# Bounds of the second MLP weights from sums of squares, taken in the first product, and more low pieces of u on GpSimd

## The chip, the cores and the metric

The kernel runs on one core of one Trainium2 chip. The metric is the device time of an execution in microseconds. A core has TensorE (PE, with its weight loads PEld), VectorE (DVE), ScalarE (ACT), GpSimd (POOL) and SyncE (SP), whose queue issues nearly all DMAs here. Each engine works through its own instructions in the order in which they were written down when the program was built.

## The reference

One block of a streaming encoder over x of 1024 x 1024: RMSNorm, two groups of attention heads, an output projection with residual, and then the part that the change is about:

```python
n2 = rms_norm(h, norm2_g[layer])                       # 1024 x 1024
u = jnp.square(jax.nn.relu(jnp.einsum('bsd,df->bsf', n2, w_ff1[layer])))   # 1024 x 4096
h = h + jnp.einsum('bsf,fd->bsd', u, w_ff2[layer])     # 4096 -> 1024
return rms_norm(h, final_norm_g)
```

All inputs and the output are float32. The kernel may compute in another way as long as the output agrees.

## The kernel before, in words

The attention and the output projection take the first 440 us or so and are not touched. The rest is the MLP, in two products.

Both products multiply 2 x 2 blocks with seven block products instead of eight (Strassen's scheme in Winograd's form), numbered p = 1 to 7. Each float32 operand of a block product is split into a high and a low fp16 piece, and `mm3` makes three matmuls of them: high x high, high x low, low x high. So that the pieces fit into fp16, an operand is first multiplied by a power of two. For that power the kernel needs a bound of the absolute values before it can split anything.

**First product** (`prepare1`, `product1`, order in `order1`). The 4096 columns of w1 are cut in NQ = 8 blocks n of 512. Per block, four tiles `w` of 128 x 1024 are loaded (`load1`), `see1` takes the largest absolute value of each (VectorE, L1161), `scale1` spreads the largest over the partitions by a TensorE transpose (`all_w`), makes the power of two, and ScalarE scales the four tiles (L1328). `prepare1` forms the combination T of two tiles (VectorE, L1335), `split` casts the high piece W (ScalarE, L1361) and takes the low piece (GpSimd or VectorE, L1363), two steps ahead of its use. `product1` then issues 24 matmuls a step (u blocks, k, three pieces) at two-output tiles, copies or sums the partial products (tiles k and v; ScalarE L1409 to L1421, VectorE L1417 to L1433), squares the relu and stores the seven operands of u to DRAM (`ud`, by `put`), from where the second product reads them back. The stores are sent by SyncE during the next step.

**Second product** (`prepare2`, `product2`, order in `order2`). The 4096 rows of w2 are cut in four groups g of two blocks n (GQ = 2), so a group has 14 steps of 24 matmuls: p in the order 1, 5, 6, 3, 7, 2, 4, each for both n. `load2w` loads the eight w2 tiles of a group, `see2` takes the largest absolute value of each (VectorE, L1161), and for groups 1 to 3 the largest goes through DRAM (`write`, `read`: SyncE sends 512 bytes out and loads them back on all partitions) to `scale2`. For group 0 it is spread by TensorE at the end of the first product. `fetch2` loads u tiles four steps ahead into six tiles that take turns (`load2u`: three of the stage ring "ws", three of "tst"). `prepare2` is written two steps ahead of the matmuls: ScalarE casts the high piece U, and for p in 1, 2, 3, 4 scales u first and has GpSimd subtract (L1363); for p in 5, 6, 7 VectorE scales and subtracts in one operation (L1365). For w2, VectorE forms the combination Z (L1335), ScalarE casts V (L1361), VectorE takes the low piece (L1365). When a pair of steps is done, `add_up` adds a PSUM bank to the float32 accumulator C (VectorE, L1652), and the next product into that bank waits for it.

All TensorE instructions stand in program order, and so do SyncE's. The order on VectorE, ScalarE and GpSimd is set by a scheduler when the program is built, from its own idea of how long things take; at run time nothing overtakes on an engine.

Of the kernel before, what the change touches and what calls it, by code (L numbers as in the profile page):

```python
# [17 lines left out]
P = 128  # L18
# [30 lines left out]
P_UP = 14  # L49
PLACES = ((4, 0, 6, 12), (0, 10, 20, 30))  # L50
V_UP = 13
PAD = 80
X_UP, W_UP, U_UP = 7, 12, 11


# [1 line left out]
def kernel(  # L57
# [40 lines left out]
    def page(shape, name, dt=F32R):  # L98
        return main.tile(shape, dt, tag="pg", bufs=NPAGES, name=name)
# [1049 lines left out]
    class Top:  # L1149
# [10 lines left out]
        def see(self, src):  # L1160
            nc.vector.tensor_reduce(self.column(), flat(src), mybir.AxisListType.X, ALU.max, apply_absolute_value=True)  # L1161

        def gather(self):
            assert self.count == self.n
            self.top = small.tile([P, 1], F32, tag="top", bufs=3, name=f"top_{self.name}")
            nc.vector.tensor_reduce(self.top, self.cols[:, : self.n], mybir.AxisListType.X, ALU.max)
# [153 lines left out]
    def scale1(n):  # L1320
        top1[n].spread()
        e = top1.pop(n).bits()
        up1 = power(scale_tile("up1", str(n), 2), e, -1.0, 254 + W_UP)
        down1[n] = power(scale_tile("down1", str(n), 3), e, 1.0, -W_UP)
        nc.vector.tensor_tensor(down1[n], down1[n], xdown, ALU.mult)
        for b in ((0, 0), (0, 1), (1, 1), (1, 0)):
            w = w1s[(n, *b)]
            nc.scalar.activation(w, w, AF.Copy, scale=up1)  # L1328

    def page1(shape, name, dt=F32):  # L1330
        return page(shape, name, dt)
# [173 lines left out]

    def load2w(n, i, j):
        if (n, i, j) not in w2s:
            w2s[n, i, j] = page([P, 2, HALF], f"w2_{n}_{i}{j}", F32)
            src = w_ff2[n * HALF + i * 2 * P : n * HALF + (i + 1) * 2 * P, j * HALF : (j + 1) * HALF]
            queue[0].dma_start(w2s[n, i, j], src.rearrange("(a p) c -> p a c", p=P))  # L1510
        return w2s[n, i, j]

    reads = {
        1: ((0, 0),), 5: ((0, 1), (0, 0)), 6: ((1, 1),), 3: ((1, 1),), 7: ((1, 1), (0, 1)), 2: ((1, 0),), 4: ((1, 0),),
# [15 lines left out]
    top2, up2, uup, udown, down2 = {}, {}, {}, {}, {}  # L1530

    def see2(g, tiles):
        if g not in top2:
            top2[g] = Top(f"w2_{g}", NQ + NQ // GQ + g, 4 * GQ)
        for tile2 in tiles:
            top2[g].see(w2s[tile2])
        if top2[g].count == 4 * GQ:
            top2[g].gather()

    def scale_of_u(g, spread=True):  # L1540
        if spread:
# [3 lines left out]
        udown[g] = power(scale_tile("udown", str(g), 4), e, 2.0, -127 - U_UP)  # L1545

    def scale2(g):
        if g == 0:
            top2[g].spread()
        e = top2.pop(g).bits(-30)  # L1550
        up2[g] = power(scale_tile("up2", str(g), 2), e, -1.0, 254 + W_UP)
        down2[g] = power(scale_tile("down2", str(g), 2), e, 1.0, -W_UP)
        nc.vector.tensor_tensor(down2[g], down2[g], udown[g], ALU.mult)

    ops2, made_b, ready2 = {}, {}, set()

    def prepare2(at):
        if at >= len(order2) or order2[at][1:] in ready2:
            return
        g, p, n = order2[at]  # L1560
        ready2.add((p, n))
        alloc = page if at <= 3 * GQ else page3
        high = lambda name: page16([P, 2, 2, HALF], name, alloc)
        temp = lambda name: alloc([P, 2, HALF], name, F32)
        a = u2s.pop((n, p))
        b = second_operands(lambda i, j: w2s[n, i, j], made_b.setdefault(n, {}), p, f"Z{n}_{p}", dve, temp)
        ops2[n, p] = (
            split(a, f"U{n}_{p}", pool if p in (1, 2, 3, 4) else dve, high, uup[g]), split(b, f"V{n}_{p}", dve, high, up2[g])
        )

    queue[0] = InOrder(nc.sync)
    for at, (n, p) in enumerate(order1):
        if p == (1 if n > 1 else 5) and n:
            load1(n + 1)
        ahead1 = at + (AHEAD1 + 1 if at < AT_ONCE else AHEAD1)

        behind = (n, p) == (0, 2)
# [12 lines left out]
        if p == 3 and n and n % GQ == 0:  # L1590
            scale_of_u(n // GQ - 1)
        if (n, p) in ((NQ - 2, 4), (NQ - 1, 1)):
            for tile2 in blocks2(0)[(p == 1) * 4 :][:4]:
                load2w(*tile2)
        if n == NQ - 1:
            if p in (5, 6):
                see2(0, blocks2(0)[(p == 6) * 4 :][:4])
            if p == 6:
                for i in range(LOAD2 - 1):
                    fetch2(i)  # L1600
            if p == 3:
                scale2(0)
            if p in (7, 2):
                prepare2({7: 0, 2: 1}[p])
    while stores:
        stores.pop(0)()
    mp_.close()
# [112 lines left out]
    for at, (g, p, n) in enumerate(order2[:-GQ]):  # L1720
# [2 lines left out]
        fetch2(at + LOAD2)  # L1723
        step = at % (7 * GQ)
        if g + 1 < NQ // GQ:
            loads = (0, 1, 2, 3) if g else (1, 2, 4, 5)
            if step in loads:
                for tile2 in blocks2(g + 1)[2 * loads.index(step) :][:2]:
                    load2w(*tile2)
            if step - 3 in loads:  # L1730
                see2(g + 1, blocks2(g + 1)[2 * loads.index(step - 3) :][:2])
            if step in (8, 10):
                (top2[g + 1].write if step == 8 else top2[g + 1].read)()
            if step == 12:
                scale2(g + 1)
        if g + 1 == NQ // GQ and step == 0:
            down, up = down2[g], scale_tile("up", "", 1)
            nc.vector.reciprocal(up, down)
        if g == 0 and step in (1, 3, 6):
            last = NQ // GQ - 1  # L1740
            {1: topu[last].write, 3: topu[last].read, 6: lambda: scale_of_u(last, False)}[step]()
        prepare2(at + AHEAD2)
        if at in (0, 1, 3, 9):
            load_acc(*into[{0: 1, 1: 5, 3: 6, 9: 4}[at]])
# [122 lines left out]
```

## Time and profile before

| what | value |
|---|---|
| median of 3 runs (lowest, highest) | 1069.95 us (1069.53, 1072.73) |
| the profiled execution | 1074.07 us, of which the span is 1072.3 |
| mean granted TensorE clock | 0.982 |
| busy: PE, DVE, ACT, POOL | 1009.7, 801.3, 655.4, 402.4 us |
| first product | from about 436 to 746 us |
| second product | from about 746 to 1064 us |
| DMA | 184 MB, mean 172 GB/s |

The page counts busy time per engine over the span, the chain that ended last, and groups of equal instructions with their mean duration and the idle time in front of them ("<-DVE C" means that the wait ended when VectorE had written C). A timeline row gives start, duration, engine, line, operation, output <- inputs, size, count, and in brackets the idle time before it. A row of windows gives, for a stretch, its length and the busy time of PE, PEld, DVE, ACT and POOL with instruction counts, the granted clock, the share of DMA and its GB/s. In the names, `f` is a PSUM tile of the first product, `f_a`, `f_b`, `f_c` are the chains of the second, `tops_w` and `top_w` are the maxima of a weight, `u` is a loaded operand of u, `ud` its place in DRAM.

### The profile page before, as it was taken

To read this page: it belongs to the slowest core of one execution; us is meant where nothing else is said; L and a number is where in the kernel's file an instruction comes from. 1 tells how busy PE (TensorE), PEld (TensorE's weight loads), DVE (VectorE), ACT (ScalarE), POOL (GpSimd) and SP (SyncE) were. 2 spreads that over 40 slices of the span, in tenths; PEclk is the share of its full clock that TensorE was granted. 3 is DMA by queue.
4 is the path that set the end of the run, shared out by engine and by line. 5 is a ranking of instruction groups with operands and counts; after the bars stand their busy time and mean duration, and the time that the engine had idled before them with its cause. 6 is when DMAs were issued, how large, how long until landed. Compare 5 with 4: busy or idle time off the path is not lost. (4 is left out here: it accounts for less than half of the span.)

```text
span 1072.3 us, 13955 instructions
## 1 busy us (share of the span) xinstructions
PE 1009.7 (94%) x4815; PEld 593.6 (55%) x4815; DVE 801.3 (75%) x1293; ACT 655.4 (61%) x1033; POOL 402.4 (38%) x327
## 2 busy tenths in 40 slices
PE   9999999999878999899999999998898799999997
PEld 7888887777656777544444444443343344444443
DVE  5577787877767465895767776777796978979886
ACT  7676766676666757755765566456264545446546
POOL 0466674244344634113533543361042214126113
PEclk9999999999989999899999999998999899999999
DMA  9854538999999954105634552473968557334204
GB/s 351 243 134 119 147 75 190 196 220 194 248 224 257 211 220 145 46 20 177 216 109 147 196 189 89 173 271 121 305 266 231 203 101 269 104 81 138 79 1 157
DMA packets 142726, 184.04 MB, mean 172 GB/s; under 512 B 78656, under 2 KB 96576, under 8 KB 142656
## 3 DMA queue, kind: packets, MB, share of 16 engines
q1 hardware_dynamic: 142512, 182.89, 58.7%
q8 instruction: 38, 0.62, 0.3%
q14 instruction: 32, 0.26, 0.1%
q10 hardware_dynamic: 144, 0.26, 0.1%
HBM read 103.43 MB, written 42.99 MB: 137 GB/s over the span
## 5 line engine op out<-in xcount | busy, mean ns | idle before, releaser
L169 PE MATMUL f<-X,W 128*128 128x512 f16 x1344 | 296.6, 383 | 0.9 <-DVE topf L1419 0.7
L169 PEld LDWEIGHTS <-U 128*128 128x128 f16 x1356 | 133.0, 98 | 186.9 <-issue 26.7
L169 PEld LDWEIGHTS <-W 128*128 128x128 f16 x1344 | 132.4, 99 | 161.6 <-issue 6.7
L169 PE MATMUL f_a<-V,U 128*128 128x512 f16 x756 | 168.2, 381 | 12.8 <-DVE C L1652 9.1
L1363 POOL TENSOR_TENSOR U<-u,U 128x1024 f16<-128x1024 f32 x32 | 78.0, 2444 | 239.9 <-ACT U L1361 137.1
L1363 POOL TENSOR_TENSOR W<-T,W 128x1024 f16<-128x1024 f32 x29 | 63.2, 2180 | 96.6 <-ACT W L1361 96.6
L169 PE MATMUL f_c<-V,U 128*128 128x512 f16 x384 | 86.9, 386 | 9.3 <-DVE C L1652 5.5
L1363 POOL TENSOR_TENSOR W<-w,W 128x1024 f16<-128x1024 f32 x23 | 55.3, 2403 | 84.4 <-ACT W L1361 84.4
L1359 ACT ACTIVATE u<-u,uup 128x1024 f32<-128x1024 f32 x32 | 36.5, 1144 | 74.0 <-DMA u<-ud 72.1
L1161 DVE TENSOR_REDUCE tops_w<-w 128x1 f32<-128x1024 f32 x64 | 75.8, 1208 | 7.2 <-DMA w<-in_w_ff_dram 6.9
L169 PE MATMUL op_A<-w_o,y 128*128 128x512 f32 x192 | 58.8, 434 | 8.5 <-DVE ts_vB L431 5.2
L1361 ACT ACTIVATE W<-T 128x1024 f16<-128x1024 f32 x32 | 33.6, 1050 | 48.6 <-DVE T L1335 48.5
L618 ACT ACTIVATE P_B<-P_B,nm_B 128x640 f32<-128x640 f32 (+2 forms) x64 | 44.2, 691 | 30.2 <-DVE nm_B L615 14.9
L863 DVE SCALAR_TENSOR_TENSOR H_B<-P_B,rc_B,H_B 128x640 f16<-128x640 f32 (+2 forms) x64 | 52.5, 848 | 10.5 <-ACT H_B L858 10.1
L1365 DVE SCALAR_TENSOR_TENSOR V<-Z,up,V 128x1024 f16<-128x1024 f32 x32 | 47.8, 1494 | 12.4 <-ACT V L1361 12.4
L169 PE MATMUL ip_qB<-nT,w_qB 128*128 128x512 f32 x192 | 53.8, 406 | 1.1 <-DVE t_kB L405 1.0
L169 PE MATMUL ip_kB<-nT,w_kB 128*128 128x512 f32 x192 | 53.7, 404 | 0.0
L1361 ACT ACTIVATE V<-Z,up 128x1024 f16<-128x1024 f32 x32 | 36.4, 1138 | 27.0 <-DVE Z L1335 21.8
L169 PE MATMUL ip_vB<-nT,w_vB 128*128 128x512 f32 x192 | 51.2, 400 | 0.0
L169 PE MATMUL ip_qA<-nT,w_qA 128*128 128x512 f32 x192 | 50.3, 396 | 0.4 <-DVE VA L175 0.4
L1420 ACT ACTIVATE k<-k,down 128x1024 f32<-128x1024 f32 x24 | 27.5, 1144 | 37.1 <-DVE topf L1419 37.1
L169 PE MATMUL op_B<-w_o,y 128*128 128x512 f32 x192 | 48.4, 407 | 0.2 <-ACT o L1053 0.2
(276 smaller groups left out, 1996.8 us busy)
## 6 DMA issues: line engine op xcount, KB each, us to landing
w<-in_w_ff_dram SPq DMA_DIRECT2D x64, 512.0 KB, 7.9
u<-ud SPq DMA_DIRECT2D x56, 512.0 KB, 5.9
ud<-k SPq DMA_DIRECT2D x48, 512.0 KB, 3.1
KkB<-t_kB SPq DMA_DIRECT2D x32, 256.0 KB, 5.3
xr<-in_x_dram SPq DMA_DIRECT2D x8, 512.0 KB, 9.3
st_o<-in_w_out_dram SPq DMA_DIRECT2D x8, 512.0 KB, 4.8
h<-in_x_dram SPq DMA_DIRECT2D x8, 512.0 KB, 5.0
hB<-h SPq DMA_DIRECT2D x8, 512.0 KB, 2.6
```

The source lines that it names most:

```text
L169: pe(nc.tensor.matmul(*args, **kw))
L618: nc.scalar.activation(pr, pr, AF.Exp, bias=nm, scale=-1.0, accum_out=sm)
L863: nc.vector.scalar_tensor_tensor(lo, q, rc, hi, ALU.mult, ALU.subtract)
L1161: nc.vector.tensor_reduce(self.column(), flat(src), mybir.AxisListType.X, ALU.max, apply_absolute_value=True)
L1359: nc.scalar.activation(full, full, AF.Copy, scale=up)
L1361: nc.scalar.activation(w[0], full, AF.Copy, scale=1.0 if up is None else up)
L1363: engine.tensor_tensor(w[1], full, w[0], ALU.subtract)
L1365: engine.scalar_tensor_tensor(w[1], full, up, w[0], ALU.mult, ALU.subtract)
L1420: nc.scalar.activation(v, v, AF.Relu, scale=down1[n])
```

## The change

The bounds of w2 are no longer maxima in the second product. From the ninth step of the first product on, `look2` loads the w2 tiles of all four groups one after the other into the stage ring (tiles m), two steps later ScalarE squares a tile in place and sums the squares along each partition (`see_squares`), and the largest sum of a group is spread by TensorE two steps after its last tile. `bits_of_root` turns it into the power of two at or below its root; the root is no less than any absolute value in the group, and usually some times larger. So all w2 tiles are loaded once more, 32 loads of 512 KB, and the weights that the second product uses are loaded as before, group 0 later than before (at steps 1 and 5 of the last block), the others one tile per step at steps 4 to 11 of the group before. The writes and reads through DRAM of groups 1 to 3 go. The scale of the sums, `down2`, is made at step 1 of its group from `wdown`.

In `prepare2`, GpSimd now takes the low piece of u for every p but 5, so also for p = 6 and 7, each with a scaling by ScalarE ahead. The scaling of w1's four tiles moves from `scale1` into `scaled1`, called by `prepare1` for the tiles that it needs. A padding tile shrinks, which moves no instruction. The write and read of the last maximum of u move from steps 1, 3, 6 to steps 4, 7, 10.

On ScalarE in the first product, around the scaling of w1 for block n = 6 (k_6 and k_5 are partial products of block 5, w_6 the tiles of w1), before:

```order
L1361 ACTIVATE W_4_6370<-T_4_6368 128x1024
L1420 ACTIVATE k_6_6328<-k_6_6328,down_5_6145 128x1024
L1421 ACTIVATE k_6_6328<-k_6_6328 128x1024
L1420 ACTIVATE k_5_6297<-k_5_6297,down_5_6145 128x1024
L1328 ACTIVATE w_6_00_6225<-w_6_00_6225,up_6_6408 128x1024
```

and now, with m_5 tiles of w2:

```order
L1381 ACTIVATE W_4_6472<-T_4_6470 128x1024
L1165 ACTIVATE m_5_00_6394,tops_w_2_6220<-m_5_00_6394 128x1024
L1165 ACTIVATE m_5_01_6427,tops_w_2_6220<-m_5_01_6427 128x1024
L1165 ACTIVATE m_5_11_6468,tops_w_2_6220<-m_5_11_6468 128x1024
L1441 ACTIVATE k_6_6425<-k_6_6425,down_5_6217 128x1024
L1442 ACTIVATE k_6_6425<-k_6_6425 128x1024
L1441 ACTIVATE k_5_6391<-k_5_6391,down_5_6217 128x1024
L1348 ACTIVATE w_6_00_6317<-w_6_00_6317,up_6_6510 128x1024
```

Three squares stand between the cast of W_4 and the relu of k_6, which was next before.

On ScalarE at the seam of the two products (k_5 and k_1 are partial products of block 7, v its last one; u and U, V belong to the second product), before:

```order
L1420 ACTIVATE k_6_6883<-k_6_6883,down_7_6687 128x1024
L1359 ACTIVATE u_1_6891<-u_1_6891,uup_5557 128x1024
L1421 ACTIVATE k_6_6883<-k_6_6883 128x1024
L1359 ACTIVATE u_1_6893<-u_1_6893,uup_5557 128x1024
L1361 ACTIVATE U_1_6973<-u_1_6891 128x1024
L1361 ACTIVATE V_1_6977<-w_0_00_6767,up_0_6935 128x1024
L1361 ACTIVATE U_1_7009<-u_1_6893 128x1024
L1361 ACTIVATE V_1_7013<-w_1_00_6811,up_0_6935 128x1024
L1361 ACTIVATE U_5_7072<-u_5_6895,uup_5557 128x1024
L1361 ACTIVATE V_5_7075<-Z_5_7070,up_0_6935 128x1024
L1420 ACTIVATE k_5_6847<-k_5_6847,down_7_6687 128x1024
```

and now, from k_5 to v:

```order
L1441 ACTIVATE k_5_6980<-k_5_6980,down_7_6821 128x1024
L1165 ACTIVATE m_7_10_7024,tops_w_3_6676<-m_7_10_7024 128x1024
L1442 ACTIVATE k_5_6980<-k_5_6980 128x1024
L1379 ACTIVATE u_1_7026<-u_1_7026,uup_5577 128x1024
L1379 ACTIVATE u_1_7028<-u_1_7028,uup_5577 128x1024
L1381 ACTIVATE U_1_7100<-u_1_7026 128x1024
L1381 ACTIVATE V_1_7104<-w_0_00_6944,up_0_5768 128x1024
L1441 ACTIVATE k_1_6941<-k_1_6941,down_7_6821 128x1024
L1381 ACTIVATE U_1_7136<-u_1_7028 128x1024
L1381 ACTIVATE V_1_7140<-w_1_00_6985,up_0_5768 128x1024
L1381 ACTIVATE U_5_7213<-u_5_7030,uup_5577 128x1024
L1381 ACTIVATE V_5_7216<-Z_5_7211,up_0_5768 128x1024
```

The relu of k_5 stood behind all of the U's and V's and now stands ahead of them, with the last square between it and its own squaring; the square of k_1, the relu of v and the square of v follow V_5.

On ScalarE in group 1 of the second product, from the first U_5 on (up_1 is the group's scale), before:

```order
L1361 ACTIVATE U_5_7637<-u_5_7551,uup_6099 128x1024
L1361 ACTIVATE V_5_7640<-Z_5_7635,up_1_7558 128x1024
L1361 ACTIVATE U_5_7677<-u_5_7594,uup_6099 128x1024
L1361 ACTIVATE V_5_7680<-Z_5_7675,up_1_7558 128x1024
L1359 ACTIVATE u_3_7709<-u_3_7709,uup_6099 128x1024
L1361 ACTIVATE U_6_7717<-u_6_7629,uup_6099 128x1024
```

and now:

```order
L1381 ACTIVATE U_5_7756<-u_5_7684,uup_6166 128x1024
L1381 ACTIVATE V_5_7759<-Z_5_7754,up_1_6266 128x1024
L1379 ACTIVATE u_3_7826<-u_3_7826,uup_6166 128x1024
L1379 ACTIVATE u_3_7863<-u_3_7863,uup_6166 128x1024
L1379 ACTIVATE u_7_7900<-u_7_7900,uup_6166 128x1024
L1381 ACTIVATE U_5_7794<-u_5_7717,uup_6166 128x1024
L1381 ACTIVATE V_5_7797<-Z_5_7792,up_1_6266 128x1024
L1379 ACTIVATE u_7_7935<-u_7_7935,uup_6166 128x1024
L1381 ACTIVATE U_6_7830<-u_6_7752 128x1024
```

Scalings of u_3 and u_7, tiles that are used four to eight steps later, now stand ahead of the second U_5.

The diff, cut to what the text speaks of:

```diff
+        def see_squares(self, src):
+            src = flat(src)
+            nc.scalar.activation(src, src, AF.Square, accum_out=self.column())
...
+        def bits_of_root(self, least):
+            e = self.bits(2 * least)
+            i = e.bitcast(I32)
+            nc.vector.tensor_scalar(i, i, float(1 << 23), 0.5, ALU.add, ALU.mult)
+            nc.vector.tensor_scalar(i, i, 0xFF << 23, None, ALU.bitwise_and)
+            nc.vector.tensor_scalar(i, i, 1.0, float(63 << 23), ALU.mult, ALU.add)
+            return e
...
-        for b in ((0, 0), (0, 1), (1, 1), (1, 0)):
-            w = w1s[(n, *b)]
-            nc.scalar.activation(w, w, AF.Copy, scale=up1)
+        to_scale1[n] = up1, [(0, 0), (0, 1), (1, 1), (1, 0)]
+
+    def scaled1(n, *blocks):
+        up1, left = to_scale1[n]
+        for b in blocks:
+            if b in left:
+                left.remove(b)
+                w = w1s[(n, *b)]
+                nc.scalar.activation(w, w, AF.Copy, scale=up1)
...
+        scaled1(n, *{1: ((0, 0), (0, 1)), 5: ((0, 1), (1, 1)), 6: ((1, 1), (1, 0))}.get(p, ((1, 0), (0, 1), (1, 1))))
...
+    to_see = [tile2 for g in range(NQ // GQ) for tile2 in blocks2(g)]
+    on_way, to_scale = [], []
+
+    def look2(at, load):
+        if to_scale and to_scale[0][0] + 2 <= at:
+            scale2(to_scale.pop(0)[1])
+        if on_way and on_way[0][0] + 2 <= at:
+            _, g, w = on_way.pop(0)
+            if g not in top2:
+                top2[g] = Top(f"w2_{g}", NQ + NQ // GQ + g, 4 * GQ)
+            top2[g].see_squares(w)
+            if top2[g].count == 4 * GQ:
+                top2[g].gather()
+                to_scale.append((at, g))
+        if load and to_see:
+            n, i, j = to_see.pop(0)
+            on_way.append((at, n // GQ, fetch_w2(stage([P, 2, HALF], f"m2_{n}_{i}{j}"), n, i, j)))
...
     def scale2(g):
-        if g == 0:
-            top2[g].spread()
-        e = top2.pop(g).bits(-30)
+        top2[g].spread()
+        e = top2.pop(g).bits_of_root(-30)
...
-            split(a, f"U{n}_{p}", pool if p in (1, 2, 3, 4) else dve, high, uup[g]), split(b, f"V{n}_{p}", dve, high, up2[g])
+            split(a, f"U{n}_{p}", dve if p == 5 else pool, high, uup[g]), split(b, f"V{n}_{p}", dve, high, up2[g])
...
-        if (n, p) in ((NQ - 2, 4), (NQ - 1, 1)):
-            for tile2 in blocks2(0)[(p == 1) * 4 :][:4]:
-                load2w(*tile2)
+        if at > 7:
+            look2(at, p not in (1, 7))
         if n == NQ - 1:
-            if p in (5, 6):
-                see2(0, blocks2(0)[(p == 6) * 4 :][:4])
+            if p in (1, 5):
+                for tile2 in blocks2(0)[(p == 5) * 4 :][:4]:
+                    load2w(*tile2)
...
-            loads = (0, 1, 2, 3) if g else (1, 2, 4, 5)
-            if step in loads:
-                for tile2 in blocks2(g + 1)[2 * loads.index(step) :][:2]:
-                    load2w(*tile2)
-            if step - 3 in loads:
-                see2(g + 1, blocks2(g + 1)[2 * loads.index(step - 3) :][:2])
-            if step in (8, 10):
-                (top2[g + 1].write if step == 8 else top2[g + 1].read)()
-            if step == 12:
-                scale2(g + 1)
+            if step in range(4, 12):
+                load2w(*blocks2(g + 1)[step - 4])
+        if step == 1:
+            scale_sums(g)
```

More of the change, by code (lines that the diff above doesn't have):

```diff
@@ L51 @@
 V_UP = 13
-PAD = 80
+PAD = 32
 X_UP, W_UP, U_UP = 7, 12, 11
@@ L1507, in load2w, with fetch_w2 @@
         if (n, i, j) not in w2s:
[L1508 to L1510 removed]
+            w2s[n, i, j] = fetch_w2(page([P, 2, HALF], f"w2_{n}_{i}{j}", F32), n, i, j)
         return w2s[n, i, j]
+    def fetch_w2(dst, n, i, j):
+        src = w_ff2[n * HALF + i * 2 * P : n * HALF + (i + 1) * 2 * P, j * HALF : (j + 1) * HALF]
+        queue[0].dma_start(dst, src.rearrange("(a p) c -> p a c", p=P))
+        return dst
     reads = {
@@ L1528, in blocks2 @@
         return [(n, i, j) for n in range(g * GQ, (g + 1) * GQ) for i, j in ((0, 0), (0, 1), (1, 1), (1, 0))]
[L1530 to L1538, printed above, removed]
+    top2, up2, wdown, uup, udown, down2 = {}, {}, {}, {}, {}, {}
+    to_see = [tile2 for g in range(NQ // GQ) for tile2 in blocks2(g)]
[14 more added lines that the diff above has]
+            on_way.append((at, n // GQ, fetch_w2(stage([P, 2, HALF], f"m2_{n}_{i}{j}"), n, i, j)))
     def scale_of_u(g, spread=True):
@@ L1600 @@
                     fetch2(i)
-            if p == 3:
-                scale2(0)
             if p in (7, 2):
                 prepare2({7: 0, 2: 1}[p])
+    assert not to_see and not on_way and not to_scale
     while stores:
```

15 lines of the change are left out of this document (9 added, 6 removed).

## The prediction

> **What bounds the kernel now.** I read the page first, then TensorE's waits, its timeline around the longest of them, and the groups of VectorE, ScalarE and GpSimd in the second product. TensorE is busy for nearly the whole span, so only its idle time and its slow stretches can be won.
>
> ```profile
> PE 1009.7 (94%) x4815; PEld 593.6 (55%) x4815; DVE 801.3 (75%) x1293; ACT 655.4 (61%) x1033; POOL 402.4 (38%) x327
> ...
> PE f_a L169 <- DVE C L1652: 9.1, 7, 2.7
> PE all_w L172 <- DVE top_w L1166: 5.8, 1, 5.8
> ...
> PE f_c L169 <- DVE C L1652: 5.5, 1, 5.5
> PE f_c L169 <- DVE V L1365: 3.2, 2, 2.2
> PE f_a L169 <- DVE V L1365: 2.9, 3, 1.9
> ...
> PE f_b L169 <- DVE V L1365: 0.7, 1, 0.7
> PE f_a L169 <- ACT V L1361: 0.7, 1, 0.7
> ...
> PE f_c L169 <- ACT V L1361: 0.4, 1, 0.4
> ```
>
> These are TensorE's waits from 420 us on (total, times, longest): 28.3 us in these rows, nearly all for VectorE in the second product or at its seam. Matmuls right behind long gaps are slow, too:
>
> ```profile
> 728.40 17.93 PE L169 MATMUL f<-X,W 128*128 128x512 f16 x72
> ...
> 764.92 5.12 PE L169 MATMUL f_c<-V,U 128*128 128x512 f16 x23 [2.24 <-DVE V L1365]
> ...
> 844.42 12.74 PE L169 MATMUL f_c<-V,U 128*128 128x512 f16 x48 [5.46 <-DVE C L1652]
> 859.81 11.88 PE L169 MATMUL f_a<-V,U 128*128 128x512 f16 x48 [2.65 <-DVE C L1652]
> 871.53 10.52 PE L169 MATMUL f_c<-V,U 128*128 128x512 f16 x48
> ```
>
> 48 matmuls (two steps, 24 each) normally take 10.52; behind 5.46 of idling they take 2.2 more, behind 2.65, 1.4 more; the 72 behind the 5.8 wait take 17.93 against 15.8. The first product has no such waits. By stages (PE, PEld, DVE, ACT, POOL busy):
>
> ```profile
> 633.50:670.00 36.50, 36.50 (x171) 16.53 (x170) 25.98 (x30) 22.37 (x23) 15.95 (x8) 1.00 0.45 159
> ...
> 820.00:892.00 72.00, 61.15 (x264) 26.46 (x263) 63.12 (x59) 38.91 (x37) 19.49 (x8) 0.93 0.62 190
> ```
>
> One column block of the first product fills TensorE; one group of the second leaves it 11 us idle while VectorE is busy for 63 of 72.
>
> **The change, part by part.** Gains have a plus.
>
> *Work moved.* The 32 maxima over w2 leave VectorE (24 in the second product), 16 low pieces of u go from VectorE to GpSimd, and each of these 16 costs ScalarE one more scaling:
>
> ```profile
> L1652 DVE SCALAR_TENSOR_TENSOR C<-f_a,down,C 128x1024 f32<-128x1024 f32 x30 | 37.7, 1273 | 0.0
> L1365 DVE SCALAR_TENSOR_TENSOR V<-w,up,V 128x1024 f16<-128x1024 f32 x22 | 37.2, 1695 | 3.8 <-ACT V L1361 3.8
> L1365 DVE SCALAR_TENSOR_TENSOR U<-u,uup,U 128x1024 f16<-128x1024 f32 x23 | 30.1, 1309 | 21.8 <-ACT U L1361 21.7
> L1161 DVE TENSOR_REDUCE tops_w<-w 128x1 f32<-128x1024 f32 x24 | 28.7, 1208 | 3.8 <-DMA w<-in_w_ff_dram 3.7
> ...
> L1363 POOL TENSOR_TENSOR U<-u,U 128x1024 f16<-128x1024 f32 x30 | 72.8, 2432 | 231.8 <-ACT U L1361 128.9 <-issue 51.1 <-DMA w<-in_w_ff_dram 41.9
> ...
> L1359 ACT ACTIVATE u<-u,uup 128x1024 f32<-128x1024 f32 x30 | 34.2, 1144 | 74.0 <-DMA u<-ud 72.1 <-DVE C L1652 1.7
> ```
>
> VectorE loses 24 x 1.21 + 16 x 1.31 = 50 us in the second product, about 15 of the 63 in a group with maxima. ScalarE gains 4 x 1.14 = 4.6 a group on 39, GpSimd 4 x 2.43 = 9.7 on 19: both stay far below 72. Hence the waits for C should go but for what the order of work causes.
> - Group 0's late VectorE backlog: 5.46 + 2.65 + 2.2 + 1.4 of slow matmuls: **+11.7**.
> - The waits for V are 7.9 together; 2.7 of them are at the seam (next but one item). The other 5.2 lie in group 0, where maxima stand between the V's and where SyncE waits for a maximum with the u loads queued behind it:
>
> ```profile
> SPq L150 <- DVE top_w L1166: 32.2, 3, 18.1
> ```
>
> These three writes and their reads are gone; I keep 0.3: **+4.9**.
> - Groups 1 to 3 wait 9.1 - 2.65 = 6.4 for C. The last 0.8 is the tail's own; I keep 4.0 in all, because ScalarE's new order is more tightly tied to reloads of u (third rival): **+2.4**.
>
> *The seam.* The spread that made TensorE wait 5.8 now comes from work done in the first product: 5.8 + 2.2 of slow clock, **+8.0**. What is late next is ScalarE. The product's last step, squared, must pass through four VectorE sums and a store before the second tile u_5 is loaded:
>
> ```profile
> 747.51 1.06 ACT L1421 ACTIVATE v<-v 128x1024 f32<-128x1024 f32 x1
> ...
> 752.42 1.23 DVE L1433 TENSOR_TENSOR k<-k,k 128x1024 f32<-128x1024 f32 x1
> ...
> 754.04 1.34 SPq L150 DMA_DIRECT2D u<-ud  x2
> ...
> 760.07 1.15 ACT L1361 ACTIVATE U<-u,uup 128x1024 f16<-128x1024 f32 x1 [11.51 <-DMA u<-ud]
> ```
>
> Now the first product ends at 746.3 (728.40 + 17.93) and the square 2.2 later, since ScalarE did the U's and V's during TensorE's wait. Without that wait they stand in the way: from the end of step p=7 (10.4 before the product's end) come a sum and a relu (2.4), then twelve operations at about 1.03, then v's relu and square (2.15): the square is done 6.5 behind the end, 4.3 later. The load still lands 6.0 behind its issue. Z_6 now goes ahead of the pair U_5, V_5, which earns 1.1 back while the load flies. So the wait at 762 to 765 grows from 2.7 to 5.2 (2.7 + 4.3 - 1.1 - 0.7 for a later start), and the matmuls behind it lose 1.9 (between the 1.4 and 2.2 above): 5.2 + 1.9 - 2.7 = 4.4, **-4.4**. The first V and U of the second product come 0.7 late by the same count: **-0.7**. Bounds: 0 (ScalarE keeps up) to -8.
>
> *The first product* gets 32 squares. The nearest row is the square with a sum over a row of h:
>
> ```profile
> L1222 ACT ACTIVATE h<-op_B x8: 1010/1024/1035, 392.5 to 436.7; 128x1024 f32<-128x1024 f32 x8
> L1222 ACT ACTIVATION_READ_ACCUMULATOR h<-op_B x8: 191/194/223, 393.4 to 437.6; 128x1 f32 x8
> ```
>
> 1.15 with its read-out. Five in a block of 36.4 make 5.8 on top of 22.4: 28 of 36, so the total fits. But three of them stand, in the order, just ahead of the scaling of the next w1:
>
> ```profile
> 649.20 1.06 ACT L1361 ACTIVATE W<-T 128x1024 f16<-128x1024 f32 x1 [3.93 <-DVE T L1335]
> ...
> 655.88 1.15 ACT L1420 ACTIVATE k<-k,down 128x1024 f32<-128x1024 f32 x1 [2.83 <-DVE topf L1419]
> 656.93 4.25 ACT L1328 ACTIVATE w<-w,up 128x1024 f32<-128x1024 f32 x4
> ...
> 663.15 2.13 POOL L1363 TENSOR_TENSOR W<-w,W 128x1024 f16<-128x1024 f32 x1 [10.68 <-ACT W L1361]
> ...
> 665.33 19.97 PEld L169 LDWEIGHTS <-W 128*128 128x128 f16 x94 [0.36 <-POOL W L1363]
> ```
>
> The low piece of W ends at 665.28 and the weight load waits for it: no slack there. Between 649.20 and 655.88 lie 6.7 us; a cast 1.06, relu 1.15, square 1.06 and three new squares 3.45 fill exactly that. A fourth square stands ahead of v's square, which starts the VectorE run that ends in the T before 649.20, so that cast itself comes up to 1.15 later. I take 0.9 a block, for six blocks (bounds 0, where the scheduler's gaps swallow it, and 2.5, where a square also waits for its load), and 0.6 for three more spreads and twelve small VectorE operations: **-6.0**. Two edits I cost at nothing. The squares' loads add 32 x 0.5 MB over some 240 us, 70 GB/s to the 159 of the block above, and DMA goes from 0.45 to about 0.65 busy: hidden behind the matmuls as long as a tile lands within the two steps (10.4 us) that the code leaves it; what lies beyond that is the second rival. And group 0's w2 now loads just ahead of its use: from about 715, behind the stores, SyncE sends eight w2 tiles, two for squares and three u, thirteen of 0.5 MB. At the rate of the fullest stretch
>
> ```profile
> 820.00:840.00 20.00, 16.22 (x73) 6.93 (x71) 18.27 (x19) 13.56 (x13) 7.25 (x3) 1.00 1.04 398
> ```
>
> each takes 1.3, so the last lands at about 732 plus its latency of 2 to 3, and the first V and U are cast at about 735: the last steps of the first product hide it, but with nothing to spare, and each further tile in that queue would put 1.3 on TensorE. The on-demand scaling of w1 leaves the four scalings of a block side by side in the order, and a smaller pad moves no instruction. The spread of a bound stands two steps behind its last square, so TensorE should not wait for it.
>
> Sum: 11.7 + 4.9 + 2.4 + 8.0 - 4.4 - 0.7 - 6.0 = **+15.9**. The profiled run took 1074.07 (span 1072.3 and 1.8 around it), which becomes 1058; it lies 4.1 above the median of the runs, so the forecast is 1069.95 - 15.9 = **1054**.
>
> **The rivals.**
> 1. *Clean.* ScalarE keeps up in the first product and at the seam: 8.0 + 5.2 + 11.7 + 5.6 - 0.6 = 29.9, so 1040. For it: 28 of 36 busy; against: the filled 6.7 us.
> 2. *The first product pays more*: squares wait for loads that share the queue with w1, 1.7 more in each of six blocks: 1064. For it: the squares' loads are issued three together behind a store; against: DMA is 0.45 busy there.
> 3. *Slower: the u ring.* load2u uses six tiles. In the new order u_7 stands ahead of the second U_5, in the tile that the first U_5 frees: between neighbouring U's then lie cast 1.14, low piece 1.31 or 2.43, landing D, scaling 1.14. Followed through a group's 14 steps (three such hops from the last U_1 to the first U_6, two to the first U_7 because the reloads of a pair overlap, one to U_2, one to U_4), there are seven D in a row and 42 us of work beside them; TensorE needs 14 x 5.2 = 72.5. With D = 3.3 that is 65, with 5.6 it is 81:
>
> ```profile
> DMA to landing us min/median/max: 3.1/3.3/11.4
> ...
> u<-ud SPq DMA_DIRECT2D x53, 512.0 KB, 5.6
> ```
>
> The first is for u from 860 to 1040, the second from 735 to 1060. At 5.6 three groups lose 8.7 each, 23 beyond the 3 that I already count: 1077, slower. It turns the sign where the three groups cost 19, 6.4 each: D = (72.5 + 6.4 - 42) / 7 = 5.3. For it: every hop is in ScalarE's fixed order, so a late tile holds up all behind it. Against it: the 5.6 holds the crowded seam, and w2 now comes one tile a step and not two.
> 4. *VectorE is held up by GpSimd.* A VectorE sum took 1.23 alone and 3.04 beside a GpSimd subtraction:
>
> ```profile
> 631.71 1.23 DVE L1427 TENSOR_TENSOR k<-v,k 128x1024 f32<-128x1024 f32 x1 [0.28 <-ACT v L1421]
> 632.97 3.04 DVE L1429 TENSOR_TENSOR v<-k,v 128x1024 f32<-128x1024 f32 x1
> ```
>
> If each of 16 new subtractions costs 1.8, 29 of the 50 us return, and of the 19.0 gained in the second product (11.7 + 4.9 + 2.4) 21/50, some 8, remain: 15.9 - 19.0 + 8.0 = 4.9, so 1065. On average V<-w is stretched by only 0.42 (1695 against C's 1273). The Trainium skill (SBUF — State Buffer, "Who interferes with whom") says that a VectorE operation with two SBUF inputs and a GpSimd one that reads SBUF block each other for the whole instruction, the later one waiting, while a reduction never does; that speaks against this change, which takes reductions away. By it up to 2.43 each, 39 us, would return, and the time would be about 1069; the mean stretch in the trace bears out much less.
>
> **How the numbers follow.** Forecast 0.55, clean 0.20, first product 0.11, u ring 0.09, held up 0.05. A time more than 0.3% (3.2 us) from 1070 can be told from no change: faster below 1066.7. Faster 0.55 + 0.20 + 0.10 with a little off, 0.85; same 0.06 (the upper ends of rivals 2 and 4); slower 0.09. The forecast's own range is 1047 to 1061. For 8 in 10 I reach to the clean case below and the first product's upper end above: 1038 to 1068.
>
> **What would show it.** Right: no wait for all_w at the seam, but 4 to 6 us for V or U about 16 us into the second product; waits for C under 5 us in all; TensorE waiting about 1 us for W at the start of each block of the first product. Wrong: u landing above 5 us in groups 1 to 3 with TensorE waiting for U, or blocks of the first product still at 36.4.

## The result, and the profile after

| kernel | median of its runs (lowest, highest) | profiled execution, span |
|---|---|---|
| before | 1070.1 us (1069.5, 1072.7) | 1074.07, 1072.3 |
| changed | 1059.55 us (1055.6, 1060.0) | 1060.0, 1058.2 |

The ratio is 0.9888 (95% interval 0.986 to 0.9917): 10.5 us faster, where the forecast was 16. The time lies 5.5 above the forecast and inside its range.

TensorE's waits from 420 us on, in the changed kernel (total, times, longest):

```profile
PE f L169 <- POOL W L1383: 6.1, 5, 1.6
PE f_c L169 <- DVE C L1686: 5.6, 1, 5.6
PE f_c L169 <- ACT V L1381: 5.4, 1, 5.4
...
PE f_a L169 <- DVE V L1385: 1.7, 1, 1.7
PE f_a L169 <- DVE C L1686: 1.0, 1, 1.0
PE f L169 <- ACT W L1381: 0.9, 2, 0.7
```

The wait for all_w is gone, and so are all waits for V in group 0 behind the seam and all waits for C in groups 0 to 2. In their place stand waits for W in the first product (7.0), a longer one for V at the seam, and one new wait for C. TensorE's timeline shows where: the start of the second product, the second u_5, and the last group.

```profile
741.29 0.38 PE L169 MATMUL f_a<-V,U 128*128 128x512 f16 x1
743.38 10.30 PE L169 MATMUL f_a<-V,U 128*128 128x512 f16 x47 [1.71 <-DVE V L1385]
...
764.26 0.58 PE L169 MATMUL f_c<-V,U 128*128 128x512 f16 x1 [5.40 <-ACT V L1381]
765.74 7.96 PE L169 MATMUL f_c<-V,U 128*128 128x512 f16 x23 [0.90 <-DVE V L1385]
...
835.70 10.52 PE L169 MATMUL f_c<-V,U 128*128 128x512 f16 x48
...
980.74 10.52 PE L169 MATMUL f_b<-V,U 128*128 128x512 f16 x48
996.91 12.13 PE L169 MATMUL f_c<-V,U 128*128 128x512 f16 x48 [5.65 <-DVE C L1686]
...
1048.90 2.78 PE L169 MATMUL end<-V,U 128*128 128x256 f16 x24
```

Between 773 and 991 us nothing holds TensorE. Then the last group stops it for 5.65, and the 48 matmuls behind take 1.6 more than the usual 10.52.

For a count by stages four more rows of before are needed:

```profile
436.37 0.32 PE L172 MATMUL all_w<-ident,top_w 128*128 128x128 f32 x1 [0.25 <-ACT F L1275]
...
746.16 10.52 PE L169 MATMUL f_a<-V,U 128*128 128x512 f16 x48
...
1002.39 10.52 PE L169 MATMUL f_b<-V,U 128*128 128x512 f16 x48
...
1063.19 2.79 PE L169 MATMUL end<-V,U 128*128 128x256 f16 x24
```

The changed kernel has the first of these at 431.81: 4.6 us of the two profiled executions' difference of 14.1 arise ahead of the MLP, which the change does not touch. They are no gain of the change: the kernel before with only its low pieces of u moved (e2 below) starts the MLP at 431.99. The other 9.5 are near the 10.5 between the medians:

| stage, from row to row | before | after | gained | forecast |
|---|---|---|---|---|
| first product and seam spread (436.37 to 746.16; 431.81 to 741.29) | 309.8 | 309.5 | 0.3 | 2.0 (8.0 - 6.0) |
| to group 1's first p = 5 (844.42; 835.70) | 98.3 | 94.4 | 3.9 | 5.3 (5.46 + 4.9 - 4.4 - 0.7) |
| to the last group's p = 2 (1002.39; 980.74) | 158.0 | 145.0 | 12.9 | 8.6 (6.25 + 2.4) |
| to the last matmuls (1063.19; 1048.90) | 60.8 | 68.2 | -7.4 | 0 |
| the end | 10.9 | 11.1 | -0.2 | 0 |

### The profile page after: what moved, and what is told of

It is laid out like the page before. It is cut to its first block, busy times and chain, and to the rows that moved or that the text cites. A ratio compares the mean times of both kernels' runs of the same rounds, so it can differ in the third digit from the quotient of the medians.

```text
span 1058.2 us, 14101 instructions
## 1 busy us (share of the span) xinstructions
PE 1003.2 (95%) x4818; PEld 591.6 (56%) x4818; DVE 760.9 (72%) x1257; ACT 702.6 (66%) x1113; POOL 453.5 (43%) x343
## 5 line engine op out<-in xcount | busy, mean ns | idle before, releaser
L1383 POOL TENSOR_TENSOR U<-u,U 128x1024 f16<-128x1024 f32 x48 | 121.0, 2531 | 180.5 <-ACT U L1381 155.3
L169 PE MATMUL f_a<-V,U 128*128 128x512 f16 x756 | 165.4, 379 | 2.7 <-DVE V L1385 1.7
L1383 POOL TENSOR_TENSOR W<-T,W 128x1024 f16<-128x1024 f32 x29 | 68.6, 2368 | 85.8 <-ACT W L1381 82.9
L1383 POOL TENSOR_TENSOR W<-w,W 128x1024 f16<-128x1024 f32 x23 | 57.8, 2516 | 93.0 <-ACT W L1381 93.0
L1379 ACT ACTIVATE u<-u,uup 128x1024 f32<-128x1024 f32 x48 | 54.6, 1143 | 63.4 <-DMA u<-ud 58.2
L1385 DVE SCALAR_TENSOR_TENSOR V<-Z,up,V 128x1024 f16<-128x1024 f32 x32 | 55.2, 1728 | 27.3 <-ACT V L1381 22.1
L1381 ACT ACTIVATE U<-u 128x1024 f16<-128x1024 f32 x48 | 50.3, 1048 | 18.1 <-PE f_a L169 6.2
L1381 ACT ACTIVATE W<-T 128x1024 f16<-128x1024 f32 x32 | 33.5, 1046 | 27.1 <-DVE T L1355 26.9
L1385 DVE SCALAR_TENSOR_TENSOR V<-w,up,V 128x1024 f16<-128x1024 f32 x24 | 43.3, 1803 | 10.9 <-ACT V L1381 7.1
L1165 ACT ACTIVATE m<-m 128x1024 f32<-128x1024 f32 x32 | 33.7, 1052 | 24.8 <-DMA m<-in_w_ff_dram 24.5
L1440 DVE CUSTOM_DVE_ANT_0 k<-f,k 128x1024 f32<-128x1024 f32 x24 | 29.2, 1219 | 27.2 <-PE f L169 26.2
```

The source lines that it names most:

```text
L169: pe(nc.tensor.matmul(*args, **kw))
L1165: nc.scalar.activation(src, src, AF.Square, accum_out=self.column())
L1379: nc.scalar.activation(full, full, AF.Copy, scale=up)
L1381: nc.scalar.activation(w[0], full, AF.Copy, scale=1.0 if up is None else up)
L1383: engine.tensor_tensor(w[1], full, w[0], ALU.subtract)
L1385: engine.scalar_tensor_tensor(w[1], full, up, w[0], ALU.mult, ALU.subtract)
```

## The experiments

Each ratio below is against the kernel before, run on the same chip beside it.

**The u part undone, and the u part alone.**

```diff
# e1_u_undone, on the changed kernel; e2_u_alone is the reverse edit on the kernel before
-  split(a, f"U{n}_{p}", dve if p == 5 else pool, high, uup[g])
+  split(a, f"U{n}_{p}", pool if p in (1, 2, 3, 4) else dve, high, uup[g])
# e3_u_undone_last, on the changed kernel
+  split(a, f"U{n}_{p}", dve if p == 5 or g == 3 and p in (6, 7) else pool, high, uup[g])
```

> The changed kernel with one part undone: the low pieces of u_6 and u_7 go back to VectorE, so 16 scalings leave ScalarE and 16 operations of 1.31 return to VectorE. Theory A (the chain of reloads of u holds up the last group: a tile of u is free only when GpSimd has subtracted, then comes the load of 3.2, then a scaling in ScalarE's order): the wait of TensorE for C at 997 us (5.65, and 1.6 of slow matmuls behind it) is gone, no other wait over 1 us in the groups: 1052 to 1053 against the 1059.55 of the change. Theory B (VectorE needed the relief): groups 1 to 3 show waits for C again, 2 to 3 each, and the 5.65 stays or grows: 1060 to 1066.

> The kernel before with that part alone: GpSimd takes the low pieces of u_6 and u_7 as well, the maxima stay. Theory A (the maxima and the seam's spread are what cost; the u part is worth little and its chain costs in the last group): the wait for all_w of 5.8 and the waits for V in group 0 stay, group 0's waits for C shrink from 8.1 by the 5.2 of VectorE work that leaves the group, the last group gains a stall of up to 7: 1064 to 1072. Theory B (the relief of VectorE is what pays): all waits for C go, 11.7 + 6.4 less: 1054 to 1058.

> The changed kernel, but in the last group alone the low pieces of u_6 and u_7 are VectorE's: 4 scalings fewer on ScalarE, 4 operations of 1.31 more on VectorE. Theory A (chain of u reloads): the stall of 5.65 + 1.6 at 997 us is gone and all before it is as it was: 7 less, 1052 to 1053. Rival (the wait for C ends late because VectorE is full there, C standing behind V in its order): the stall stays or is longer, 1059 to 1062.

Measured: undone everywhere 1053.9 us, ratio 0.9838 (0.9822 to 0.9854); undone in the last group alone 1053.6, 0.9836 (0.9819 to 0.9852); alone on the kernel before 1074.1, 1.003 (1.0018 to 1.0041). The times lie 0.6 to 2.1 above the ranges of theory A, and the waits went and came as it says. So the change is two parts of opposite sign. The bounds by squares, with all that comes with them, are worth 1.6%, 17 us; the low pieces on GpSimd cost some 6 in the changed kernel and 3 by themselves. No run separates the maxima's time on VectorE from the writes and reads through DRAM and from the times of w2's loads, which change together with it. TensorE's timeline in the last group, with everything undone (no wait, as with the last group undone), and with the u part alone (a longer stall):

```profile
992.63 10.52 PE L169 MATMUL f_c<-V,U 128*128 128x512 f16 x48
```
```profile
1010.44 12.64 PE L169 MATMUL f_c<-V,U 128*128 128x512 f16 x48 [8.37 <-DVE C L1652]
```

The rival of a full VectorE falls: four more operations for VectorE in the last group removed the wait for VectorE. The u part alone did help behind group 0 (the long wait for C there fell from 5.46 to 3.40), and lost more than that at the end.

**Why the last group stalls: order, number of tiles.** ScalarE in the changed kernel, with VectorE's answer:

```profile
970.63 1.15 ACT L1379 ACTIVATE u<-u,uup 128x1024 f32<-128x1024 f32 x1 [3.59 <-DMA u<-ud]
...
977.38 1.15 ACT L1379 ACTIVATE u<-u,uup 128x1024 f32<-128x1024 f32 x1 [3.52 <-DMA u<-ud]
...
984.16 1.15 ACT L1379 ACTIVATE u<-u,uup 128x1024 f32<-128x1024 f32 x1 [3.55 <-DMA u<-ud]
...
992.01 1.15 ACT L1379 ACTIVATE u<-u,uup 128x1024 f32<-128x1024 f32 x1 [3.77 <-DMA u<-ud]
993.06 1.13 ACT L1381 ACTIVATE V<-Z,up 128x1024 f16<-128x1024 f32 x1
```
```profile
994.28 1.28 DVE L1385 SCALAR_TENSOR_TENSOR V<-Z,up,V 128x1024 f16<-128x1024 f32 x1 [4.47 <-ACT V L1381]
995.49 2.47 DVE L1686 SCALAR_TENSOR_TENSOR C<-f_b,down,C 128x1024 f32<-128x1024 f32 x2
```

Four scalings of u wait for their load; from one to the next are 6.75, 6.8 and 7.85, and TensorE uses a step in 5.2. Each stands ahead of a cast of V that is wanted sooner. VectorE waits for that V, and the sum C, which frees TensorE's bank, stands behind it in VectorE's order. The wait for a load that stands behind all this is on ScalarE, two engines away from the "DVE C" that TensorE's row names.

```diff
# e11_in_turn: scalings and casts of U and V tied to the order of the code
+    in_turn = InOrder(nc.scalar)
...
-            nc.scalar.activation(full, full, AF.Copy, scale=up)
+            act2[0].activation(full, full, AF.Copy, scale=up)   # act2[0] is in_turn in prepare2
# e10_seven_tiles
-NPAGES = 33
+NPAGES = 32
-        return main.tile(shape, dt, tag="ws", bufs=3, name=name)
+        return main.tile(shape, dt, tag="ws", bufs=4, name=name)
-        if len(u2s_made) % 2 == 0 or len(u2s_made) == 1:
+        if len(u2s_made) % 7 in (0, 1, 2, 4):
```

> The changed kernel with GpSimd's part whole, but ScalarE's instructions of the second product's operands are tied to the order in which the code writes them: u_7's scaling stands right ahead of U_7, no longer ahead of the second U_5. Theory A1 (the stall of the last group comes from scalings that stand too early in ScalarE's order, so that each load's landing of 3 to 4 us is waited for between two neighbouring U's): the stall of 5.65 + 1.6 goes as it did when the low pieces went back: 1052 to 1054. Rival A2 (the extra work of ScalarE and GpSimd itself, or six tiles being too few whatever the order): the stall stays: 1058 to 1061.

> The changed kernel with seven tiles in turn for u in place of six (one page less for the rest). The scheduler moves u_7's scaling forward by the same tile, ahead of the first U_5 in place of the second. Theory A1 (the hop between two neighbouring U's in ScalarE's order): one tile more shortens no hop, the stall of 4 to 7 stays: 1057 to 1061. Rival A2 (too few tiles): the stall goes: 1052 to 1054.

Measured: in turn 1053.3 us, 0.9838 (0.9818 to 0.9858), with all of GpSimd's part in place. Seven tiles 1068.9, 0.9972 (0.9956 to 0.9988), slower than both ranges expected. In turn, no scaling of u between 955 and 1000 us waits for its load, though the loads take as long as in the changed kernel (median 3.2 to landing in both), and the same step of TensorE has no wait (first fence); with seven tiles it has one of 4.39, 1.7 of slow matmuls behind it (second):

```profile
991.53 10.52 PE L169 MATMUL f_c<-V,U 128*128 128x512 f16 x48
```
```profile
441.40 0.32 PE L172 MATMUL all_w<-ident,top_w 128*128 128x128 f32 x1 [0.25 <-ACT F L1287]
...
1005.44 12.21 PE L169 MATMUL f_c<-V,U 128*128 128x512 f16 x48 [4.39 <-DVE C L1686]
```

So it is the order of ScalarE's scalings and casts, which the edit ties together; with seven tiles four scalings in a row, from 978.40 on, still wait 3.2 to 4.5 for their loads and follow one another at 6.95, 7.67 and 7.52. The loss of the seven tiles is elsewhere: the MLP starts 9.6 later (441.40 against 431.81). That the page taken away is missed there was not tested by itself.

**The squares in the first product.** The start of a block in the changed kernel, on ScalarE and TensorE:

```profile
651.62 1.06 ACT L1165 ACTIVATE m<-m 128x1024 f32<-128x1024 f32 x1 [2.42 <-DMA m<-in_w_ff_dram]
...
658.50 4.25 ACT L1348 ACTIVATE w<-w,up 128x1024 f32<-128x1024 f32 x4
...
663.60 1.04 ACT L1381 ACTIVATE W<-w 128x1024 f16<-128x1024 f32 x1
```
```profile
664.69 0.60 PE L169 MATMUL f<-X,W 128*128 128x512 f16 x2 [0.74 <-ACT W L1381]
666.90 13.34 PE L169 MATMUL f<-X,W 128*128 128x512 f16 x61 [1.60 <-POOL W L1383]
```

Two candidates: the three squares' work, and the wait for their loads in front of them.

```diff
# e5_small_squares: leaves seven eighths of each tile out of the bound, the loads stay whole
             src = flat(src)
+            src = src[:, :P]
# e6_squares_moved, on e3_u_undone_last
-        if at > 7:
-            look2(at, p not in (1, 7))
+        if at > 5:
+            look2(at, p not in (5, 6, 3) or n < 3)
```

> The changed kernel with squares of the first 128 of each tile's 1024 columns only, which leaves out seven eighths of the bound; the loads of the tiles stay whole. A square takes some 0.4 in place of 1.25 with its read-out. Theory A (ScalarE's work ahead of w1's scaling makes TensorE wait for W): the waits for W, 7 to 8 in all, fall below 2, and the seam's wait for V by 1: 1052 to 1054. Rival (a square waits for its tile's load, 2.4 for the first of three, so a short square ends hardly earlier): waits for W keep 5 or more, 1057 to 1059.5.

> Base is the changed kernel with the last group's low pieces of u_6 and u_7 on VectorE (1053.6). On it the squares are moved only: w2 tiles are looked at from the sixth step on, in every step until block 2 is done, then not at p = 5, 6, 3, so that in blocks 3 to 6 one square stands between the cast of W_4 and the scaling of w1, where there were three, and block 2 has five. Theory A (work ahead of the scaling of w1): the waits for W, 8 to 9 in all, vanish in blocks 4 to 7; block 3's grows to about 4: 1048 to 1050. Rival (the squares' total work, wherever it stands, is what delays): 1053 to 1055.

Measured: short squares 1052.8 us, 0.9826 (0.9809 to 0.9842), 6.8 less than the change. In the profiles the first product, from its first matmul of f to the second product's first, takes 303.0 against 309.4. Its waits for W are 1.7 in all, though ScalarE waits for m's loads no less than in the changed kernel (28.9 against 24.5 in its groups from 470 to 745 us):

```profile
PE f L169 <- POOL W L1384: 1.7, 2, 1.3
```
```profile
L1166 ACT ACTIVATE m<-m 128x128 f32<-128x128 f32 x32 | 9.8, 305 | 29.0 <-DMA m<-in_w_ff_dram 28.9
```

So the work is the price, not the loads. Moving it earned nothing: 1053.2, 0.983 (0.9809 to 0.9851), against 1053.6 for its base. The waits changed shape: 0.65 to 0.9 in each of five blocks, 2.6 in another, and 2.3 for a scale of u. The scheduler had put the freed square to the other side of w1's scaling, still ahead of the cast of W_1 and still 1.0 long (ScalarE's timeline):

```profile
627.46 1.04 ACT L1165 ACTIVATE m<-m 128x1024 f32<-128x1024 f32 x1
...
629.44 1.04 ACT L1381 ACTIVATE W<-w 128x1024 f16<-128x1024 f32 x1
```

So no run shows whether it is the squares' place that counts or only their sum. If work ahead of W_1 is too long, the three scalings that W_1 does not need could go behind it:

```diff
# e12_w1_in_turn, on e3_u_undone_last: w_00, W_1, w_01, W_5, ... in the order of use
-                nc.scalar.activation(w, w, AF.Copy, scale=up1)
+                in_turn1.activation(w, w, AF.Copy, scale=up1)      # split's casts, too
-   {1: ((0, 0), (0, 1)), 5: ((0, 1), (1, 1)), 6: ((1, 1), (1, 0))}
+   {1: ((0, 0),), 5: ((0, 1),), 6: ((1, 1),), 3: ((1, 1),)}
```

> Base is the changed kernel with the last group's low pieces of u_6 and u_7 on VectorE (1053.6); the squares stay where they are. ScalarE's scalings of w1 and casts of W are tied to the order of their use: w_00, W_1, w_01, W_5 and so on, so that three scalings of 1.04 no longer stand between w_00 and W_1. Theory A (TensorE waits for W_1 at a block's start because ScalarE's work ahead of it is 1 to 3 too long, wherever it stands): W_1 comes 3.1 earlier, all waits for W (8 to 9 with the 1.6 between the first two and the rest of the matmuls) go: 1045 to 1047. Rival (the wait moves on to W_5, whose tile w_01 is now scaled later): waits for W of 1 to 2 at the second step of a block: 1050 to 1054.

Measured: 1062.8 us, 0.9943 (0.993 to 0.9956), against 0.9836 for its base 1.1% or 11 us slower; the expectation missed on both sides. The waits for W stayed and waits for k, which ScalarE copies out of TensorE's banks, came up (TensorE's waits, then ScalarE's timeline at the start of a block):

```profile
PE f L169 <- ACT k L1435: 7.9, 6, 1.9
PE f L169 <- POOL W L1386: 6.8, 6, 1.6
```
```profile
622.07 1.06 ACT L1165 ACTIVATE m<-m 128x1024 f32<-128x1024 f32 x1 [3.83 <-DMA m<-in_w_ff_dram]
...
630.55 1.04 ACT L150 ACTIVATE W<-w 128x1024 f16<-128x1024 f32 x1
```

The rest of a block comes later in the fixed order: T, the sums of v on VectorE, their stores, and the squares' loads, which SyncE sends behind the stores. In this block the three loads go out at 616.35 against 607.26, with TensorE only 5.3 later. The first square therefore waits 3.8, and W_1, though now two places behind w_00, is late again: TensorE waits for it at 631 us, 0.9 for the cast and 1.6 for the low piece. Which of these links leads was not taken apart further.

**The seam.** The second U_5 on ScalarE in the changed kernel, and what SyncE does meanwhile:

```profile
748.16 1.06 ACT L1442 ACTIVATE v<-v 128x1024 f32<-128x1024 f32 x1
762.02 1.15 ACT L1381 ACTIVATE U<-u,uup 128x1024 f16<-128x1024 f32 x1 [12.81 <-DMA u<-ud]
```
```profile
755.41 1.50 SPq L150 DMA_DIRECT2D u<-ud  x2
```

```diff
# e7_seam_load, on e3_u_undone_last: v and k_5 of the last block in pg2 tiles, fourth u load ahead of the stores
-            if p == 5 and n:
+            if p == 5 and 0 < n < NQ - 1:
-        v = tst([P, 2 * HALF], f"v{n}") if p == 4 else ...
+        v = (tst if n < NQ - 1 else page2)([P, 2 * HALF], f"v{n}") if p == 4 else ...
-                for i in range(LOAD2 - 1):
+                for i in range(LOAD2):
```

> Base is again 1053.6. On it v and k_5 of the last block live in other tiles, so that the second u_5 can be loaded ahead of the last block's stores; ScalarE's order is the same. Theory A (TensorE's wait for V 16 us into the second product, 4.1 + 0.9 and 2.6 of slow matmuls behind it, is the chain of v's square, four VectorE sums, a store and then the load of u_5): all of it goes, 1046 to 1048. Rival (VectorE's sums delay Z_5, V_5 and their low pieces as well, so a wait for V stays): a wait of 2 to 4 at the same place: 1050 to 1053.

Measured: 1050.5 us, 0.9804 (0.9783 to 0.9825), 3.1 less than its base, in the rival's range. In TensorE's timeline the wait of 5.0 became 0.66, but new ones followed, the next for V and then for C:

```profile
760.46 5.12 PE L169 MATMUL f_c<-V,U 128*128 128x512 f16 x23 [0.66 <-DVE V L1385]
...
767.28 10.30 PE L169 MATMUL f_a<-V,U 128*128 128x512 f16 x47 [1.48 <-DVE V L1385]
...
799.79 2.75 PE L169 MATMUL f_b<-V,U 128*128 128x512 f16 x12 [1.49 <-DVE C L1686]
```

Of the 7.6 that the wait of 5.0 and the slow matmuls behind it cost in the base, 3.1 came back. What is left is VectorE, which must still end the last block's sums before the second Z_5, for which ScalarE's cast of V_5 now waits, and which then runs without a lead:

```profile
756.91 1.15 ACT L1381 ACTIVATE V<-Z,up 128x1024 f16<-128x1024 f32 x1 [5.93 <-DVE Z L1355]
```

**Together.** e13 is e11, e12 and e7 in one; e14 is e12 and e7; e15 is e11 and e7.

> All three together, with GpSimd's whole part kept: ScalarE in turn in both products (1053.3 for the second alone) and the load of u_5 ahead of the stores. By the single runs: 1053.3 less 8 for W and less 3 for the seam: 1042 to 1044, if the parts add up. Rival (what one part frees the next wait takes, as the load of u_5 alone gained 3 of 7.6): 1046 to 1049.

> As the one before, but the second product's order is left to the scheduler and the last group's low pieces of u_6 and u_7 are VectorE's. If the parts add up, 1053.6 less 8 less 3: 1042 to 1044, the same as with GpSimd's part in turn within 1.5; if GpSimd's part in turn is worth something of its own (the waits for C in group 0 that came up with the early u_5, 1.9 and slow matmuls), 2 to 3 more than that one.

> The changed kernel whole, with two repairs: ScalarE's instructions of the second product in the order of the code (alone: 1053.3) and the second u_5 loaded ahead of the last block's stores, with v and k_5 of that block in other tiles (alone: 3.1 less on a base of 1053.6, with waits for C of 1.9 coming up in group 0). The first product is left as it is. If the parts add up: the wait of 6.5 + 0.9 at the seam goes, the waits for C in group 0 stay small since GpSimd keeps its part: 1046 to 1049. Rival (as in the run of all three, the gain at the seam goes into waits for C in group 0 and an emptier lead): 1050 to 1053.

Measured: e13 1058.7 us, 0.9905 (0.9881 to 0.993), and e14 1061.4, 0.9927 (0.9915 to 0.9939): both miss what was expected (1042 to 1044, with a rival of 1046 to 1049 for e13) and carry the loss of e12 with them: their first products take 320.1 and 321.2, where the changed kernel's takes 309.4. e15, 1048.7, 0.979 (0.9761 to 0.9819), keeps the whole change and beats it by 11 and the kernel before by 22; it cannot be told from e7. TensorE's waits from 420 us on in e15; the largest part of what is left are the first product's 6.6 for W:

```profile
PE f L169 <- POOL W L1385: 5.0, 5, 1.6
...
PE f_b L169 <- DVE C L1691: 1.9, 2, 1.5
...
PE f L169 <- ACT W L1383: 1.6, 2, 1.4
```

## Why the prediction was right, and where its sum was off

The direction and most of the size were right, and right by what was named: VectorE's maxima and the seam's spread. With the u part undone, the bounds alone gave 17 us. That this comes to 1053.9, the forecast's 1054, is luck: the forecast counted the u part as a gain. Of its signs, the wait for all_w went and the waits for W came (0.2 to 2.3 a block, in five blocks); the wait for V at the seam was 6.3 instead of 4 to 6; and the waits for C, to be under 5, came to 6.6, by the stall of the u ring, a rival that it had put at 0.09.

- **Group 0's late backlog, +11.7, and its waits for V, +4.9**: all gone, as forecast, and gone with the u part undone too, so that the bounds alone did it.
- **The seam's spread, +8.0**: gone, as forecast.
- **Groups 1 to 3, +2.4, the failing term (4.3 too much by the rows).** It kept 4.0 of scattered waits for C. The runs showed none in groups 1 and 2, and in the last group one stall of 5.65 with 1.6 behind it, and 1.0 at the tail: 8.3 against the 6.4 of before. It is the third rival's mechanism, and its place (scalings too early in ScalarE's order) is shown by putting them back in turn. The rival's count was wrong in form: it added seven hops over a group and compared 65 with 72.5. In the last group, whose order is 1, 2, 5, 6, the hops come one a step, 6.75 to 7.85 against 5.2, with loads that land in 3.2 and not the 5.3 at which the count said that the sign turns.
- **The seam's second u_5, -4.4**: the mechanism was right, the size 2.0 short. The wait grew from 2.7 to 6.3, not 5.2: v's square ended 7.9 behind the product's end, not 6.5. The slow matmuls behind it lost 2.8, not 1.9. **The first V, -0.7**, was 1.7.
- **The first product, -6.0**: right in that the squares' work on ScalarE makes TensorE wait for W, 1.7 too small by stages. The waits for W are 7.0; short squares brought back 6.8 in all. That it is the three squares ahead of w1's scaling that count is read from the order alone.
- **The sum by rows**: 11.7 + 4.9 - 1.9 + 8.0 - 6.4 - 1.7 - 7.7 = 6.9, where the stages gained 9.5. Two rows of 48 matmuls, 10.52 each, start 10.36 apart, so a stop costs 0.16 beyond its wait; from 746 to 1002 us the kernel before stops 15 times and the changed one, up to the same step, three times. That is an estimate of 1.9 of the missing 2.6; the rest is open.
- **GpSimd in VectorE's way, the fourth rival**: its stretch happened, its price did not. It took 1.8 for each subtraction. The groups of VectorE from 776 to 1035 us, in the changed kernel and with the u part undone:

```profile
L1385 DVE SCALAR_TENSOR_TENSOR V<-Z,up,V 128x1024 f16<-128x1024 f32 x28 | 49.4, 1763 | 27.3 <-ACT V L1381 22.1 <-issue 5.2
...
L1355 DVE TENSOR_TENSOR Z<-w,w 128x1024 f32<-128x1024 f32 x14 | 26.4, 1888 | 4.9 <-PE f_c L169 4.8
...
L1385 DVE SCALAR_TENSOR_TENSOR U<-u,uup,U 128x1024 f16<-128x1024 f32 x6 | 7.7, 1283 | 8.4 <-issue 5.7 <-ACT U L1381 2.7
```
```profile
L1385 DVE SCALAR_TENSOR_TENSOR V<-Z,up,V 128x1024 f16<-128x1024 f32 x28 | 38.6, 1377 | 5.7 <-ACT V L1381 5.6
...
L1385 DVE SCALAR_TENSOR_TENSOR U<-u,uup,U 128x1024 f16<-128x1024 f32 x20 | 25.6, 1280 | 17.1 <-ACT U L1381 11.2 <-issue 5.8
...
L1355 DVE TENSOR_TENSOR Z<-w,w 128x1024 f32<-128x1024 f32 x14 | 17.0, 1218 | 6.8 <-PE f_c L169 6.7
```

Fourteen subtractions fewer save VectorE 17.9, and the two groups of V and Z shown here take 20.2 longer (10.8 + 9.4). VectorE was not relieved at all: from 770 to 1040 us it is busy for 216.4 in the changed kernel and 212.7 with the u part undone. It cost no time, because VectorE had room in these groups: in turn (e11, 207.0 busy, so that some of the relief does arrive) the kernel is as fast as without GpSimd's part (1053.3 against 1053.9). So the u part, which the forecast counted as two fifths of VectorE's relief (21 of 50), was worth nothing that the runs can show even without its stall.

## What to carry to other kernels

Where a scheduler writes an engine's order down, an operation that waits for a transfer must not stand ahead of work that is wanted sooner: follow the reload of each tile through that order, step by step at the place where the hops come closest, and not as a mean over a stage. When a change has two parts, time each alone before judging it; here one gave 17 us and the other took 6 back. Mending the spot that a wait names need not pay: moving the squares, one more tile and an earlier W_1 all left the time or made it worse; where it was followed up, other work in the same order was late.

## What the runs showed of the hardware that was not expected

- Moving work from VectorE to GpSimd can leave VectorE as busy as before. V and Z, with two inputs in SBUF, went from 1377 and 1218 ns to 1763 and 1888, while the sums C, with one input in PSUM, stayed at 1273 to 1279. Taken one by one from 776 to 1035 us in the changed kernel, those of V and Z that no low piece on GpSimd overlaps take 1207 to 1284, and the others up to 3152; the six U's, with two inputs in SBUF as well, are overlapped by none and stay at 1283; the sums C take 1268 to 1284 with and without, and eight maxima of the kernel before beside a low piece 1212 on average against 1206. By the rule of the Trainium skill (SBUF — State Buffer, "Who interferes with whom"), a VectorE operation with two SBUF inputs contends with a GpSimd one that reads SBUF, and one with at most one SBUF input, outside the two-port modes, does not: these rows agree.
- How long they hold each other up depends on the order of the work: GpSimd's 48 low pieces of u took 2531 ns on average in the changed kernel and 2181 in e15, where only ScalarE's order, one load and two tiles differ.
- 48 matmuls behind a gap of 5.65 lost 1.6, with a granted clock of 0.87 from 997 to 1009 us, and 23 behind 5.40 and 0.90 lost 2.8, with 0.62 from 764 to 774: the loss behind a gap is not a fixed price.
